# Layer norms of a two-layer decoder step: scaling in place on VectorE, the shift inside the split, GpSimd's shift of the residual later

## The chip, the cores and the metric

The kernel runs on one core of one Trainium2 chip. The metric is the device time of one execution in microseconds (us), the median of several runs. Engines are called PE (TensorE matmuls), DVE (VectorE), ACT (ScalarE), POOL (GpSimd) and SP (SyncE, which issues most DMAs).

## The reference, cut to what matters

One inference step of a decoder with two layers, 512 prompt tokens and 8 single sample tokens, model width 1024, all in float32. Layer 0 mixes tokens by windowed attention, layer 1 by gated linear attention; each is followed by a gated convolutional feed-forward part of width 2816. Behind each of the four parts stands a layer norm of the residual:

```
def layer_norm(x, g, b):
    mu = jnp.mean(x, -1, keepdims=True)
    var = jnp.mean(jnp.square(x - mu), -1, keepdims=True)
    return (x - mu) * lax.rsqrt(var + LN_EPS) * g + b

for i in range(DEPTH):
    x = layer_norm(ALPHA * x + mix_i(x), ln_mix_g[i], ln_mix_b[i])
    x = layer_norm(ALPHA * x + conv_ffn_i(x), ln_ffn_g[i], ln_ffn_b[i])
```

So the result of a norm is used twice: as the input of the next matrix products, and as the residual that the next part is added to.

## The kernel before, in words

**Tiling.** Activations lie with features on the 128 partitions and tokens in the free dimension. The tokens are two groups: a with 256 prompt tokens, b with 256 prompt and 8 sample tokens. A group's residual is the tile x (x_a, x_b): 8 chunks of 128 features. Matrix products run in float32r with operands split in two: a high half, rounded by ACT, and a low half, the rest, by a subtraction on DVE (tiles xh and xl; for group a both lie in xs_a). A product (lines 164 to 195) of one unit, 128 output features by one group, adds high x high, high x low and low x high over the chunks in one of four PSUM accumulators (accp). Weights come by DMA as raw, ACT makes wh (line 158) and DVE wl (line 161).

**Order.** Units are traced in an order in which group a leads group b by four or five units (line 931), so that at the end of a phase b's last units run while a's layer norm is made, and a's first units of the next phase run while b's layer norm is made. One unit of one group is a slot. A generator that yields n is taken up again n slots later (lines 912 to 929). A planner then orders each engine's instructions: it simulates the program with a cost model and takes what is ready, by the order of tracing. `issue_after(ins)` puts what is traced under it behind `ins` in the queue of the same engine; the engines run their queues strictly in order.

**The layer norm.** `ln_chunk` (line 208) adds the last product of a part to chunk m of x and gathers the sums s1 and s2 (of x and its squares). `ln_end` (line 251) is one slot later: PE sums over the partitions by ones matrices (line 256), ACT copies the mean mu (line 261), POOL subtracts it from chunks 0 to 4 and DVE from 5 to 7 (line 263), ACT's Ln and Exp (lines 273, 274) with three DVE operations (275 to 277) give r, the reciprocal deviation. Then for each chunk: DVE multiplies by r into a tile u with two buffers (296), ACT makes the high half from u with gain and shift (297), POOL makes the new residual x from u with gain and shift (298), and DVE subtracts the high half from that x for the low half (301). `pool_mark` is POOL's last such operation; the next norm's subtractions on POOL are issued after it (264). The last norm of the program (`last`) goes another way and writes y.

**The feed-forward part.** `ffn_gate` (line 564) copies a gate product to SBUF with two columns of history in front (POOL copies them, line 202), makes the convolution on DVE (lines 580, 581) and a Gelu on ACT (line 588); `ffn_value` multiplies it with the value product (line 600), which releases that accumulator. The residual x is next touched by `ffn_down` of the first part (line 613), 12 units of each group later, or, in the linear attention, by the output projection (line 219). There POOL also adds one to the denominators of the output gate (line 859).

Of the kernel before, what the change touches and what calls it, by code (L numbers as in the profile page):

```python
# [11 lines left out]
F32 = mybir.dt.float32  # L12
F32R = mybir.dt.float32r
I32 = mybir.dt.int32
AF = mybir.ActivationFunctionType
ALU = mybir.AluOpType
# [6 lines left out]
KD = 8  # L23
# [28 lines left out]

S2P = 4
NSUB = 5

WIDE = 4

# [16 lines left out]
def parted(rows):  # L74

    return rows.rearrange("p (j t) -> p t j", t=2)
# [15 lines left out]
class Net:  # L92
# [157 lines left out]

    def ln_end(self, g, i, last=False):
        nc, n, x = self.nc, g.n, g.x
        yield 1
        e1, e2 = self.mtile("tp")[:, :n], self.mtile("pv")[:, :n]
        for e, sums, rest in ((e1, g.s1, x[:, KD - 1]), (e2, g.s2, g.q)) if last else ((e1, g.s1, None), (e2, g.s2, None)):
            nc.tensor.matmul(e, self.ones_a, sums, start=True, stop=rest is None)
            if rest is not None:
                nc.tensor.matmul(e, self.ones_a, rest, start=False, stop=True)
        t = lambda name, b=1: self.ln.tile([P, NT - 256], F32, name=name, bufs=b)[:, :n]
        mu, q, nv, r = t("mu"), t("msq"), t("nv"), t("r")  # L260
        nc.scalar.copy(mu, e1)
        nc.scalar.activation(q, e1, AF.Square)
        sub = lambda eng, m: eng.tensor_tensor(x[:, m], x[:, m], mu, op=ALU.subtract)
        with self.tc.issue_after(self.pool_mark) if self.pool_mark else ExitStack():
            for m in range(2, KD) if last else range(NSUB):
                sub(nc.gpsimd, m)
        nvi = nc.vector.scalar_tensor_tensor(nv, q, LN_EPS, e2, op0=ALU.subtract, op1=ALU.subtract)
        with self.tc.issue_after(nvi.ins):
            if last:
                nc.vector.tensor_tensor(x[:, 0:2], x[:, 0:2], mu.unsqueeze(1).broadcast_to([P, 2, n]), op=ALU.subtract)  # L270
            else:
                sub(nc.vector, NSUB)
        nc.scalar.activation(r, nv, AF.Ln, scale=-1.0)
        nc.scalar.activation(r, r, AF.Exp, scale=-0.5)
        nc.vector.tensor_tensor(q, r, r, op=ALU.mult)
        nc.vector.scalar_tensor_tensor(q, q, 0.5, nv, op0=ALU.mult, op1=ALU.mult)  # L276
        ri = nc.vector.scalar_tensor_tensor(r, q, 1.5, r, op0=ALU.add, op1=ALU.mult)
        sc = lambda m: self.par[:, C_LNG + i * KD + m:C_LNG + i * KD + m + 1]
        bi = lambda m: self.par[:, C_LNB + i * KD + m:C_LNB + i * KD + m + 1]
        if last:  # L280
            for m in range(0, KD, 2):
                xp = x[:, m:m + 2]
                nc.vector.tensor_tensor(xp, xp, r.unsqueeze(1).broadcast_to([P, 2, n]), op=ALU.mult)
                for j in (m, m + 1):
                    if j in (0, 2, 4, 5, 7):
                        nc.scalar.activation(x[:, j], x[:, j], AF.Identity, scale=sc(j), bias=bi(j))
                    else:
                        nc.vector.tensor_scalar(x[:, j], x[:, j], sc(j), bi(j), op0=ALU.mult, op1=ALU.add)
                nc.sync.dma_start(out=self.O["y"][:, m:m + 2, g.c0:g.c0 + n], in_=xp)
            return  # L290
        for m in range(KD):
            if m > NSUB:
                with self.tc.issue_after(ri.ins):
                    sub(nc.vector, m)
            u = t("u", 2)
            nc.vector.tensor_tensor(u, x[:, m], r, op=ALU.mult)  # L296
            nc.scalar.activation(g.xh[:, m], parted(u), AF.Identity, scale=sc(m), bias=bi(m))
            ts = nc.gpsimd.tensor_scalar(x[:, m], u, sc(m), bi(m), op0=ALU.mult, op1=ALU.add)  # L298
            if m == KD - 1:
                self.pool_mark = ts.ins  # L300
            nc.vector.tensor_tensor(g.xl[:, m], parted(x[:, m]), g.xh[:, m].bitcast(F32), op=ALU.subtract)  # L301

    def load_x(self, i, m0, m1):
        g, nc = self.groups[i], self.nc
# [259 lines left out]
    def ffn_gate(self, g, u, layer, j, q):  # L564
        nc, n = self.nc, g.n
        ps, lo = self.product2(g, u, g.xs, g.xh, g.xl, j >= WIDE)
        w = lambda i: self.par[:, C_CW + (layer * 3 + i) * NF + j:C_CW + (layer * 3 + i) * NF + j + 1]
        cb = self.par[:, C_CB + layer * NF + j:C_CB + layer * NF + j + 1]
        a = self.fp.tile([P, 2 + NT - 256], F32, name="aext", bufs=2)
        if g.i == 0:  # L570
            nc.gpsimd.memset(a[:, 0:2], 0.0)
        else:
            self.pcopy(a[:, 0:2], self.hist[:, j])
        nc.scalar.copy(a[:, 2:2 + n], ps)
        t = lambda name: self.fp.tile([P, NT - 256], F32, name=name, bufs=2)
        c = t("conv")
        if lo is not None:
            nc.vector.tensor_tensor(a[:, 2:2 + n], a[:, 2:2 + n], lo, op=ALU.add)  # L578
        nc.scalar.activation(c[:, :256], ps[:, :256] if lo is None else a[:, 2:258], AF.Identity, scale=w(2), bias=cb)
        nc.vector.scalar_tensor_tensor(c[:, :256], a[:, 1:257], w(1), c[:, :256], op0=ALU.mult, op1=ALU.add)  # L580
        nc.vector.scalar_tensor_tensor(c[:, :256], a[:, 0:256], w(0), c[:, :256], op0=ALU.mult, op1=ALU.add)
        if g.i == 0:
            self.pcopy(self.hist[:, j], a[:, 256:258])
        else:
            nc.vector.scalar_tensor_tensor(c[:, 256:n], a[:, 258:2 + n], w(2), self.base[:, j], op0=ALU.mult, op1=ALU.add)
            self.pcopy(self.nconv_p[:, j], a[:, 256:258])
            self.pcopy(self.nconv_s[:, j, :, 1], a[:, 258:2 + n])
        nc.scalar.activation(c[:, :n], c[:, :n], AF.Gelu)
        g.gate = c
        yield 0  # L590

# [368 lines left out]
    def run(self):  # L960
        nc = self.nc
        self.plan()
        self.nu, self.extra, self.close_wx = WSLOTS, {}, False
        self.attn_open()
        self.later, self.slot, self.seq, self.pool_mark = [], 0, 0, None
        for i, u in self.order():
            g = self.groups[i]
            _, _, f, a, pre = self.units[u]
            if i == 0 and pre:
                pre()  # L970
                if pre != self.gla_open:
                    for _ in range(EXTRA):
                        self.next_unit(True)
            self.slot += 1
            self.resume(f(g, u, *a))
            if i == 1:
                x = self.extra.pop(u, False)
                if not x or self.more(u):
                    self.next_unit(x)
                elif not self.extra:  # L980
                    self.close_wx = True
            if self.close_wx and self.fp is None:
                self.close(self.wx_cm)
                self.close_wx = False
            self.due()
        while self.later:
            self.slot += 1
            self.due()
# [115 lines left out]
```

## Time and profile before

| | us |
|---|---|
| median of 3 timed runs | 1148.62 (1147.16 to 1149.75) |
| the profiled execution | 1146.73 |
| its span in the profile | 1144.7 |
| PE busy | 1104.2 (96%) |
| DVE busy | 794.5 (69%) |
| ACT busy | 575.6 (50%) |
| POOL busy | 326.4 (29%) |

The profile is of one execution. An engine's busy time is the union of its instructions; times of day are counted from the start of the span. The mean granted TensorE clock of the span was 0.992 of full speed. The views used below are the busy time of each engine in windows, the waits (who waited for whose instruction, and how long in all), the chain of work that ended last, the timeline of one engine, and the instructions of one line.

### The profile page before, as it was taken

The page shows a single profiled execution, that of the slowest core. Times are in us where ns is not written, and L with a number is a line of the kernel's source. Part 1 is how long each engine was busy: PE and PEld are TensorE (multiplying, and loading weights), DVE is VectorE, ACT ScalarE, POOL GpSimd, SP SyncE. Part 2 cuts the span into 40 slices and gives each one's busy share as a digit, 9 for nine tenths or more (in the row PEclk, how much of TensorE's full clock was granted, in tenths as well). Part 3 has the DMA queues.
Part 4 walks back from the last instruction along what each step waited for, and adds up shares of the span by engine and source line. Part 5 has one row for each costly group of instructions (what it writes and reads, how often), then busy time and mean ns, then how long its engine had stood idle before and what let it go on. Part 6 is the DMA issues. An engine that isn't in the chain of part 4 may idle for free.

```text
span 1144.7 us, 22953 instructions
## 1 busy us (share of the span) xinstructions
PE 1104.2 (96%) x8806; PEld 1055.2 (92%) x8806; DVE 794.5 (69%) x1663; ACT 575.6 (50%) x1253; POOL 326.4 (29%) x556
## 2 busy tenths in 40 slices
PE   8999899999999999999899999989999999999995
PEld 8997798999999999998899999888999999999994
DVE  7897589655665566668867777799655665566657
ACT  5677457534553245435545556456524553245433
POOL 4575568100110011357300101287100110011344
PEclk9999999999999999999899999999999999999998
DMA  7553031323323233243124355341333232232222
GB/s 241 149 183 90 13 111 56 111 93 123 99 93 111 92 99 105 74 133 110 38 89 147 117 177 162 133 145 62 105 96 127 93 106 98 92 111 93 74 63 75
DMA packets 53789, 122.82 MB, mean 107 GB/s; under 512 B 6792, under 2 KB 27312, under 8 KB 53680
## 3 DMA queue, kind: packets, MB, share of 16 engines
q1 hardware_dynamic: 51664, 119.61, 32.4%
q10 hardware_dynamic: 2016, 1.75, 0.5%
q8 instruction: 69, 1.13, 0.4%
q14 instruction: 40, 0.33, 0.1%
HBM read 108.67 MB, written 8.47 MB: 102 GB/s over the span
## 4 chain that ended last, share of the span: by engine, by line
PE 70%; DVE 12%; DMA 6%; ACT 4%; POOL 4%; issue 4%; SPq 0%; ACTq 0%; DVEq 0%; POOLq 0%
PE accp L191 15%; PE accp L174 14%; PE accp L173 14%; PE accp L175 14%; PE accp L192 8%; DMA vb<-dv 3%; DVE wl L161 2%; POOL x_b L298 1%; DVE sgla L845 1%; DMA qs<-hl 1%; ACT wh L158 1%; POOL x_a L298 1%; DVE u L296 1%; PE pv L494 1%; DVE msq L276 1%
## 5 line engine op out<-in xcount | busy, mean ns | idle before, releaser
L161 DVE TENSOR_TENSOR wl<-raw,wh 128x1024 fp32r<-128x1024 f32 (+2 forms) x189 | 231.4, 1226 | 106.7 <-ACT wh L158 105.2
L158 ACT ACTIVATE wh<-raw 128x1024 fp32r<-128x1024 f32 (+2 forms) x185 | 191.9, 1037 | 215.0 <-PE accp L174 196.8
L173 PE MATMUL accp<-xh_b,wh 128*128 128x264 f32 x976 | 271.7, 279 | 2.5 <-DVE hprod L600 2.5
L174 PE MATMUL accp<-xl_b,wh 128*128 128x264 f32 x976 | 271.3, 278 | 0.2
L175 PE MATMUL accp<-xh_b,wl 128*128 128x264 f32 x976 | 270.8, 278 | 0.0
L191 PE MATMUL accp<-xs_a,wh 128*128 128x512 f32 x576 | 196.3, 382 | 0.0
L173 PEld LDWEIGHTS accp<-xh_b,wh 128*128 128x128 f32 x976 | 185.0, 190 | 3.5 <-DVE hprod L600 2.9
L174 PEld LDWEIGHTS accp<-xl_b,wh 128*128 128x128 f32 x976 | 184.9, 189 | 3.1 <-DVE xl_b L301 0.6
L175 PEld LDWEIGHTS accp<-xh_b,wl 128*128 128x128 f32 x976 | 184.8, 189 | 0.8 <-issue 0.6
L192 PE MATMUL accp<-xs_a,wl 128*128 128x256 f32 x576 | 145.4, 273 | 0.0
L173 PE MATMUL accp<-hh_b,wh 128*128 128x264 f32 x480 | 133.7, 279 | 3.3 <-ACT hh_b L198 3.3
L174 PE MATMUL accp<-hl_b,wh 128*128 128x264 f32 x480 | 134.3, 280 | 0.0
L175 PE MATMUL accp<-hh_b,wl 128*128 128x264 f32 x480 | 133.3, 278 | 0.0
L191 PEld LDWEIGHTS accp<-xs_a,wh 128*128 128x128 f32 x576 | 109.1, 189 | 11.4
L173 PE MATMUL accp<-xs_a,wh 128*128 128x256 f32 x400 | 112.3, 287 | 5.6 <-DVE x_b L219 2.1
L174 PE MATMUL accp<-xs_a,wh 128*128 128x256 f32 x400 | 112.4, 283 | 3.2 <-DVE xs_a L301 2.9
L192 PEld LDWEIGHTS accp<-xs_a,wl 128*128 128x128 f32 x576 | 110.2, 191 | 1.9
L175 PE MATMUL accp<-xs_a,wl 128*128 128x256 f32 x400 | 111.0, 280 | 0.7 <-DVE wl L161 0.5
L173 PEld LDWEIGHTS accp<-hh_b,wh 128*128 128x128 f32 x480 | 91.3, 190 | 3.8 <-ACT hh_b L198 3.6
L174 PEld LDWEIGHTS accp<-hl_b,wh 128*128 128x128 f32 x480 | 91.3, 190 | 1.4 <-issue 0.3
L175 PEld LDWEIGHTS accp<-hh_b,wl 128*128 128x128 f32 x480 | 91.3, 190 | 0.2
L202 POOL COPY hist<-aext 128x2 f32<-128x2 f32 x44 | 8.9, 203 | 284.4 <-DVE aext L578 281.3
(320 smaller groups left out, 2495.3 us busy)
## 6 DMA issues: line engine op xcount, KB each, us to landing
raw<-in_w_up SPq DMA_DIRECT2D x88, 512.0 KB, 3.4
raw<-in_w_down SPq DMA_DIRECT2D x32, 512.0 KB, 3.4
raw<-in_w_gla SPq DMA_DIRECT2D x24, 512.0 KB, 3.4
raw<-in_w_mix_o SPq DMA_DIRECT2D x16, 512.0 KB, 4.1
raw<-in_w_down SPq DMA_DIRECT2D x16, 384.0 KB, 3.1
qs<-hl SPq DMA_DIRECT2D x64, 64.0 KB, 2.1
sgla<-in_state_gla SPq DMA_DIRECT2D x16, 256.0 KB, 2.8
vb<-dv SPq DMA_DIRECT2D x16, 256.0 KB, 3.7
```

Source lines behind the costliest of these rows:

```text
L158: nc.scalar.activation(h[:, c], r[:, c], AF.Copy)
L161: nc.vector.tensor_tensor(l[:, c], r[:, c], h[:, c].bitcast(F32), op=ALU.subtract)
L173: nc.tensor.matmul(o, h[:, ks], xh, start=k == 0, stop=False)
L174: nc.tensor.matmul(o, h[:, ks], xl, start=False, stop=False)
L175: nc.tensor.matmul(o, l[:, ks], xh, start=False, stop=k == nt - 1)
L191: both = lambda: nc.tensor.matmul(o, h[:, ks], in_turn(rs[:, k].rearrange("p t q j -> p t (q j)")), start=k == 0, stop=last)
L192: low = lambda: nc.tensor.matmul(o[:, :P], l[:, ks], in_turn(rh[:, k]), start=False, stop=False)
L276: nc.vector.scalar_tensor_tensor(q, q, 0.5, nv, op0=ALU.mult, op1=ALU.mult)
L296: nc.vector.tensor_tensor(u, x[:, m], r, op=ALU.mult)
L298: ts = nc.gpsimd.tensor_scalar(x[:, m], u, sc(m), bi(m), op0=ALU.mult, op1=ALU.add)
L494: mm = nc.tensor.matmul(pv[64 * v:64 * v + 64, b * P:(b + 1) * P], self.vtok[:, kb, 64 * v:64 * v + 64], parts[v][w][:, b], start=i == 0, ...
L845: late(nc.vector.scalar_tensor_tensor(s[:, j], vb[:, j], kraw[:, b:b + 1], s[:, j], op0=ALU.mult, op1=ALU.add))
```

## The change

In the norms that are not the last, the tile u goes. DVE multiplies x in place by gain and r in one operation; ACT makes the high half from x with the shift as its bias; DVE makes the low half as (x + shift) - high half. POOL adds the shift to x in place in a generator step that is taken up 14 slots later. POOL's mean subtractions are no longer issued after a mark. Group b's `ln_end` is taken up in the same slot, not one later. The Gelus of the first three gates of each feed-forward part are issued after the latest Exp of a norm.

```diff
+LATEB = 14
@@ ln_end
-        yield 1
+        yield 0 if g.i and not last else 1
...
-        with self.tc.issue_after(self.pool_mark) if self.pool_mark else ExitStack():
-            for m in range(2, KD) if last else range(NSUB):
-                sub(nc.gpsimd, m)
+        for m in range(2, KD) if last else range(NSUB):
+            sub(nc.gpsimd, m)
...
-        nc.scalar.activation(r, r, AF.Exp, scale=-0.5)
+        self.exp = nc.scalar.activation(r, r, AF.Exp, scale=-0.5).ins
...
         for m in range(KD):
             if m > NSUB:
                 with self.tc.issue_after(ri.ins):
                     sub(nc.vector, m)
-            u = t("u", 2)
-            nc.vector.tensor_tensor(u, x[:, m], r, op=ALU.mult)
-            nc.scalar.activation(g.xh[:, m], parted(u), AF.Identity, scale=sc(m), bias=bi(m))
-            ts = nc.gpsimd.tensor_scalar(x[:, m], u, sc(m), bi(m), op0=ALU.mult, op1=ALU.add)
-            if m == KD - 1:
-                self.pool_mark = ts.ins
-            nc.vector.tensor_tensor(g.xl[:, m], parted(x[:, m]), g.xh[:, m].bitcast(F32), op=ALU.subtract)
+            nc.vector.scalar_tensor_tensor(x[:, m], x[:, m], sc(m), r, op0=ALU.mult, op1=ALU.mult)
+            nc.scalar.activation(g.xh[:, m], parted(x[:, m]), AF.Identity, bias=bi(m))
+            nc.vector.scalar_tensor_tensor(g.xl[:, m], parted(x[:, m]), bi(m), g.xh[:, m].bitcast(F32), op0=ALU.add, op1=ALU.subtract)
+        yield LATEB
+        for m in range(KD):
+            nc.gpsimd.tensor_scalar(x[:, m], x[:, m], 1.0, bi(m), op0=ALU.mult, op1=ALU.add)
@@ ffn_gate
-        nc.scalar.activation(c[:, :n], c[:, :n], AF.Gelu)
+        with self.tc.issue_after(self.exp) if j < 3 else ExitStack():
+            nc.scalar.activation(c[:, :n], c[:, :n], AF.Gelu)
```

## Rows read from the trace of the kernel before

**Rows 1.** Windows: length, busy PE, PEld, DVE, ACT, POOL (instructions), granted clock, DMA share, GB/s.
```profile
160.00:180.00 20.00, 17.65 (x151) 17.14 (x150) 19.37 (x38) 12.13 (x20) 15.24 (x13) 1.00 0.39 129
180.00:200.00 20.00, 18.24 (x155) 17.45 (x154) 17.81 (x38) 13.84 (x29) 16.65 (x23) 1.00 0.09 27
200.00:220.00 20.00, 20.00 (x160) 19.39 (x159) 14.93 (x30) 11.59 (x22) 3.23 (x12) 1.00 0.38 120
...
520.00:540.00 20.00, 17.51 (x148) 16.82 (x147) 19.07 (x39) 11.97 (x21) 15.25 (x13) 1.00 0.40 132
540.00:560.00 20.00, 16.79 (x109) 14.96 (x109) 16.37 (x37) 11.21 (x24) 11.77 (x14) 0.83 0.03 7
...
760.00:780.00 20.00, 16.64 (x139) 15.90 (x138) 20.00 (x38) 12.21 (x20) 16.38 (x13) 1.00 0.37 126
780.00:800.00 20.00, 18.25 (x154) 17.48 (x153) 17.82 (x38) 13.89 (x29) 16.50 (x23) 1.00 0.09 27
```

**Rows 2.** PE's waits, grouped: us in total, times, the longest.
```profile
PE accp L174 <- DVE xs_a L301: 2.9, 2, 1.5
PE accp L173 <- DVE hprod L600: 2.5, 2, 1.3
PE accp L173 <- DVE x_b L219: 2.1, 2, 1.1
...
PE accp L672 <- DVE xl_b L301: 1.5, 2, 1.0
PE accp L672 <- DVE xs_a L301: 1.3, 1, 1.3
PE accp L173 <- DVE x_b L217: 1.1, 1, 1.1
```

**Rows 3.** The chain that ended last, from 150 to 205: start, us, what.
```profile
191.44 4.12 POOL x_b L298 x4
```

**Rows 4.** POOL's timeline, 155 to 200: start, us, what, idle before and its releaser.
```profile
166.75 6.39 POOL L298 TENSOR_SCALAR x_a<-u,par 128x256 f32<-128x256 f32 x4 [3.22 <-DVE u L296]
...
177.82 3.08 POOL L298 TENSOR_SCALAR x_a<-u,par 128x256 f32<-128x256 f32 x2 [0.70 <-DVE u L296]
180.87 4.33 POOL L263 TENSOR_TENSOR x_b<-x_b,mu 128x264 f32<-128x264 f32 x5
```

**Rows 5.** DVE's timeline, the same stretch.
```profile
166.22 0.76 DVE L296 TENSOR_TENSOR u<-x_a,r 128x256 f32<-128x256 f32 x2
166.89 1.22 DVE L161 TENSOR_TENSOR wl<-raw,wh 128x1024 fp32r<-128x1024 f32 x1
...
169.26 0.43 DVE L301 TENSOR_TENSOR xs_a<-x_a,xs_a 128x256 fp32r<-128x256 f32 x1 [0.47 <-POOL x_a L298]
...
171.03 1.42 DVE L161 TENSOR_TENSOR wl<-raw,wh 128x1024 fp32r<-128x1024 f32 x1
```

**Rows 6.** Line 301: what DVE, idle before it, waited for (us, times).
```profile
  POOL x_a L298: 2.1, 5
  POOL x_b L298: 0.8, 2
```

**Rows 7.** Instructions of lines 580, 277, 298, 558: min/median/max ns, first to last start.
```profile
L580 DVE SCALAR_TENSOR_TENSOR conv<-aext,par,conv x88: 473/482/617, 186.4 to 1091.8; 128x256 f32<-128x256 f32 x88
...
L277 DVE SCALAR_TENSOR_TENSOR r<-msq,r x8: 412/847/873, 164.9 to 1134.9; 128x256 f32<-128x256 f32 x4, 128x264 f32<-128x264 f32 x4
...
L298 POOL TENSOR_SCALAR x_b<-u,par x24: 651/1110/1322, 186.3 to 794.9; 128x264 f32<-128x264 f32 x24
...
L558 POOL TENSOR_TENSOR base<-sconv,par x2: 495/534/573, 140.4 to 755.1; 128x176 f32<-128x176 f32 x2
```

**Rows 8.** ACT's timeline, 155 to 200.
```profile
177.45 0.38 ACT L261 COPY mu<-tp 128x264 f32<-128x264 f32 x1 [0.45 <-PE tp L256]
...
180.37 0.42 ACT L274 ACTIVATE r<-r 128x264 f32<-128x264 f32 x1
...
187.47 1.28 ACT L588 ACT_TABLE_LOAD   x1
```

More of the change, by code (lines that the diff above doesn't have):

```diff
@@ L964, in run @@
         self.attn_open()
-        self.later, self.slot, self.seq, self.pool_mark = [], 0, 0, None
+        self.later, self.slot, self.seq = [], 0, 0
         for i, u in self.order():
```

## The prediction

> **What bounds the kernel now.** The first view to read is the busy time by windows of 20 us, TensorE (PE) first. In the middle of a feed-forward phase PE is busy for 20.00 of 20 us while VectorE (DVE) has some 25% left [rows 1], as in the window from 200. PE loses time in three places: 160 to 200, 520 to 560 and 760 to 800, with 4.11, 5.70 and 5.11 us not busy (20 minus the PE column, summed over two windows), together 14.9 us. In the window from 540 the granted clock is also 0.83 on average: with two levels that is 6.8 of the 20 us at the lower, 1.2 GHz (0.17 / 0.5 x 20), which costs up to 3.4 us of matmul time. DVE is at 16.4 to 20.0 of 20 us there. So about 18 us is all that there is to win at these places. They are the three layer norms that are not the last, each for group a and then for group b.
>
> Second, PE's waits, grouped [rows 2]. Three kinds carry these places: waits that end with the low half of a normalized chunk (L301: 2.9, 1.5 and 1.3, in sum 5.7 us), waits for an accumulator that the gate-times-value product has to release (L600, 2.5 us), and waits for one that the residual add has to release (L219 and L217, 2.1 and 1.1 us). All end on DVE.
>
> Third, what DVE waits for. Across the first layer norm the chain of waits runs through GpSimd (POOL): four of its scalings (L298) in a row make up 4.12 us of it [rows 3]. POOL's own timeline says why [rows 4]: beside a busy DVE four scalings take 6.39 us, 1.6 each, and the subtractions of the mean for group b begin at 180.87, when group a's last scaling ends, because line 264 puts them behind it. Group a's first chunk is multiplied by r at 166.22 and its low half starts only at 169.26, DVE having sat idle 0.47 us for POOL [rows 5]. Over all layer norms DVE idled 2.9 us in front of L301 for L298 [rows 6].
>
> **The change part by part.**
> (a) The low half no longer reads what POOL wrote. Per chunk there were, and are, two DVE operations and one on ScalarE (ACT); POOL's scaling leaves the chain between them, and so does the two-buffer tile u. Group a's first chunk took 3.04 us from 166.22 to 169.26; the two DVE operations (0.4 us each) with ACT's (0.6) between them would take half of that. I count the whole of the 5.7 us that PE waited for L301. From below this could be 0, if DVE's backlog lets nothing come earlier; from above it is 5.7.
> (b) Group b's mean subtractions are no longer behind group a's scalings. POOL could start when the mean is there, at 177.83 (177.45 and 0.38 us [rows 8]), where two scalings of group a now start [rows 4]: 3.0 us before 180.87. That moves group b's chunks and, with them off DVE, the convolutions and products of the first gates: the 2.5 us of waits for L600 go. Bounds: 0 (r of group b comes from DVE, not from POOL) and 2.5.
> (c) The waits for the residual add stay as they are, 3.2 us: they come from the order in DVE's queue.
> (d) The stretch at the lower clock followed stop-and-go matmuls. With part of those stops gone I take half of it, 1.7 us. Bounds 0 and 3.4; the nearest rows say no more than that one of the three places has it and the two others don't [rows 1].
> (e) The price: both new DVE operations take a per-partition operand from the parameter tile. A scalar_tensor_tensor of 128x256 took at least 0.473 us with such an operand (L580) and 0.412 with a constant (L277) [rows 7]; the tensor_tensor that they replace is as quick as the latter, 0.76 us for two that overlap [rows 5]. That is 0.061 us more for each of 2 operations x 8 chunks x 6 norms = 96, or 5.9 us of DVE time. Where DVE is full half of it reaches PE by my reckoning: 2.9 us. Bounds 0 and 5.9.
> (f) POOL's 48 operations come back 14 slots later and change x in place. Alone or beside DVE they take 0.65 to 1.3 us (L298 on group b) [rows 7], so some 53 us of POOL in all, and they slow DVE a little: splitting weights took 1.22 us and 1.42 us in two places beside such scalings [rows 5], so up to 0.2 each, 9.6 us of DVE. They are not wanted before x is next added to, in the first down projection or the next output projection. If they land after the window, PE is at 20.00 of 20 there and DVE's free quarter hides them; if the planner pulls them forward, the contention is what it is today. Zero, with 9.6 as the price if DVE had no room.
> (g) Group b's statistics matmuls are written one slot earlier. DVE's sums, not the slot, release them, so zero; a slot, about 24 matmuls at 20/160 us [rows 1], is 3 us, the most that it could give or take.
> (h) The Gelus of the first three gates are put behind the layer norm's Exp in ACT's queue. They are behind it already: Exp at 180.37, the Gelu table at 187.47 [rows 8]. Zero; the cover is 7 us wide, and if it went two more table loads of 1.28 us would be at stake in each feed-forward phase. In the last norm only the order behind an old mark goes: zero.
>
> The sum: -5.7 - 2.5 - 1.7 + 2.9 = -7.0 us. The profiled execution took 1146.73 us (span 1144.7, 2.0 outside), so 1139.7 for such a one; the median of the timed runs is 1.9 above it, so 1141.6 there. By each part's bounds the likeliest case lies between -11.6 and 0; I expect it within 1137 to 1146.
>
> The Trainium skill speaks against (f). Its GPSIMD Engine Reference, under Key points, says that GpSimd shares its SBUF interfaces with VectorE and contends with VectorE instructions that have two SBUF inputs. The trace agrees: 1.6 us a scaling beside DVE in rows 4 against 0.65 at best in rows 7. By that rule moving the scalings into the feed-forward phase, where DVE has many two-input operations, keeps their cost rather than removing it; the sum above does not credit any relief for it.
>
> **The rivals.**
> R1, no change: DVE's total work is the bound and only the order of it changes. For it: DVE is within 0 to 1 us of full in the windows from 160, 520 and 760 [rows 1], and (e) adds 5.9 us against the 2.9 us of idle time that it loses [rows 6] and what the missing waits let it do. Then the time is 1148.6 plus or minus 2: +3.0 of DVE, less about as much as is put off until after the place, where DVE has room. Against it: the weight splits of 1.2 us in these places aren't needed at once, and can wait.
> The Trainium skill has a rule on R1's side: VectorE: DVE Perf Modes, under Rules for kernel authors, advises to cut the number of DVE operations rather than fuse them. Here 96 stand for 96; by that rule DVE gains nothing. No row can show the new pair itself.
>
> R2, slower: the late scalings block POOL's queue. They are issued eight at a time per group; if the eight stand together, 8 x 1.11 us (median of L298 on group b [rows 7]) = 8.9 us during which the tiny copies of the gate's history, or the denominators of the linear attention's gate, stand behind them, DVE waits in order for those, and PE's accumulators are not released. Of four accumulators two are filled or read, so the other two give about 2 x 3.0 = 6 us of cover. The excess, 2.9 us, comes six times: +17.4, less 7, is +10.4, so 1159. It decides only from a block longer than six us. Against it: the planner puts POOL operations where POOL is idle. The feed-forward phase's base computation (L558) first ran at 140.4 [rows 7], 26 us before group a's first normalized chunk at 166.22 [rows 5], which opens that phase; and POOL is busy for only 3 of 20 us behind the place [rows 1].
>
> R3, faster still: the chunks are ready so early that the planner puts off weight splits and nearly all of the three places closes. Of the 14.9 us and 3.4 of clock, three quarters: -13.7, so 1135. For it: POOL's pace is 1.6 us a chunk today and DVE's would be 0.8. Against it: (c), and DVE at 20.
>
> **How the numbers follow.** The forecast (1137 to 1146) gets 0.52, R3 0.17, R1 0.18, R2 0.13. About 0.2%, 2.3 us, is what a measurement of this kernel can tell from no change. Below 1146.3 lie the forecast, R3 and a sixth of R1: 0.72. Above 1150.9 lies R2 and a trace of R1: 0.14. The rest, 0.14, is no change. The range from 1133 to 1151 takes in the forecast, R1 and most of R3 and leaves out R2: some 0.8.
>
> **What would show it.** Right: no wait of PE or DVE that ends at POOL's scaling; group b's mean subtractions on POOL right behind the mean, some 3 us earlier than now; PE busy 37 to 39 of 40 us in 160 to 200 and 760 to 800; the waits for L301 and L600 under 3 us together; no stretch, or a shorter one, at 0.5 clock near 550; the new DVE operations at 0.47 to 0.49 us. Wrong: the same PE stalls ending at DVE operations of another line (R1), or DVE and PE waiting for a POOL copy behind a row of eight scalings in the feed-forward phases (R2). The prediction is wrong if the three places don't shrink, or if PE falls below 19.9 of 20 in the windows right behind them.

## The result, and the profile after

Before 1148.59 us (1147.16 to 1150.63, 6 runs), after 1154.26 us (1153.72 to 1155.44, 6 runs): a ratio of 1.0048, 95% interval 1.0035 to 1.0061. By the ratio the kernel became slower by 5.5 us, where 7 us less were forecast. The profiled execution of after took 1154.34 us, its span 1152.2 (7.5 more than before) at a mean granted clock of 0.983.

The changed kernel's lines are shifted a little: L297 is the multiplication in place, L298 ACT's high half, L299 the low half, L302 POOL's later shift, L249 and L251 the sums of group b, L163 the weight split, L263 the copy of the mean, L265 the mean subtraction, L221 the residual add, L603 the gate product.

The windows of after, in the columns of [rows 1]:

```profile
160.00:180.00 20.00, 16.64 (x123) 16.45 (x122) 19.46 (x37) 11.08 (x19) 11.00 (x14) 0.83 0.32 106
180.00:200.00 20.00, 19.25 (x165) 18.73 (x165) 16.43 (x37) 11.16 (x25) 8.93 (x12) 1.00 0.17 53
200.00:220.00 20.00, 20.00 (x166) 19.58 (x165) 15.46 (x29) 13.02 (x26) 8.67 (x22) 1.00 0.36 113
520.00:540.00 20.00, 16.20 (x138) 15.71 (x137) 19.19 (x36) 11.95 (x22) 9.44 (x11) 1.00 0.31 105
540.00:560.00 20.00, 16.36 (x124) 15.25 (x123) 17.50 (x38) 7.40 (x19) 11.75 (x16) 0.95 0.09 28
560.00:580.00 20.00, 18.43 (x138) 17.64 (x138) 14.90 (x34) 11.18 (x28) 1.61 (x4) 0.88 0.21 70
760.00:780.00 20.00, 15.37 (x119) 14.88 (x118) 19.67 (x35) 11.69 (x22) 12.06 (x15) 0.91 0.33 106
780.00:800.00 20.00, 19.46 (x155) 18.97 (x154) 16.53 (x36) 11.52 (x25) 9.89 (x16) 0.92 0.26 79
```

The same three places are open, and the first window of each opened further: PE is 3.36 us short of full from 160 (2.35 before), 3.80 from 520 (2.49) and 4.63 from 760 (3.36), while the second window of the first and third closed by about 1 us (0.75 against 1.76 from 180). New is the granted clock there, 0.83 and 0.91 where it had been 1.00. From 200 on PE is at 20.00 of 20 as before; behind the second norm the loss runs on into the window from 560 (18.43, where it had been 20.00). Comparing when the same DVE instruction starts in both traces says the same: after is 1.2 us late ahead of the first norm, gains 1.8, 2.3 and 2.2 us of lateness at the three norms, and stays constant through the feed-forward phases between them (3.06 us late from 252 to 500). The 1.2 us lie in attention, in front of the first changed instruction, and are less than the 1.9 us by which the profiled execution of before was under its median; part of them goes with the clock, 0.72 on average from 132 to 144 where before had 0.86.

PE's waits of after, grouped, in the columns of [rows 2]:

```profile
PE accp L176 <- DVE xs_a L299: 7.3, 2, 3.9
PE accp L675 <- DVE xs_a L299: 3.8, 2, 3.4
PE accp L675 <- DVE xl_b L299: 3.6, 2, 2.8
```

The waits for the gate product and the residual add of [rows 2] have gone, and DVE no longer sits idle in front of a low half (2.1 and 0.8 us for POOL in [rows 6]). But the wait for the low half went from 5.7 us in all to 14.7, and the longest from 1.5 to 3.9. What DVE does in front of it, to hold against [rows 5]:

```profile
167.45 2.85 DVE L297 SCALAR_TENSOR_TENSOR x_a<-x_a,par,r 128x256 f32<-128x256 f32 x7
170.22 1.21 DVE L163 TENSOR_TENSOR wl<-raw,wh 128x1024 fp32r<-128x1024 f32 x1
171.36 0.47 DVE L297 SCALAR_TENSOR_TENSOR x_a<-x_a,par,r 128x256 f32<-128x256 f32 x1
171.75 0.42 DVE L249 TENSOR_TENSOR s_b<-s_b,x_b 128x264 f32<-128x264 f32 x1
172.10 0.42 DVE L251 TENSOR_TENSOR s_b<-s_b,sq 128x264 f32<-128x264 f32 x1
172.44 0.47 DVE L299 SCALAR_TENSOR_TENSOR xs_a<-x_a,par,xs_a 128x256 fp32r<-128x256 f32 x1
```

Before, two multiplications were issued (x2 in [rows 5]) and then none until ACT and POOL had read one of u's two buffers. The third stands behind the first low half (169.26 in [rows 5]):

```profile
169.60 0.42 DVE L296 TENSOR_TENSOR u<-x_a,r 128x256 f32<-128x256 f32 x1
```

Now seven stand in one row, then a weight split, the eighth, two sums of group b, and only then the first low half: 4.99 us behind the first multiplication instead of 3.04. DVE has no idle time in this stretch: it is not waiting for anyone, it does other work first. ACT had the first two high halves done by 168.92:

```profile
167.96 0.96 ACT L298 ACTIVATE xs_a<-x_a,par 128x256 fp32r<-128x256 f32 x2
...
185.32 0.38 ACT L263 COPY mu<-tp 128x264 f32<-128x264 f32 x1
```

With the long stops the clock fell. Windows of after cut at the changes of clock:

```profile
165.30:172.10 6.80, 4.31 (x39) 4.12 (x37) 6.80 (x17) 3.67 (x8) 0.00 (x0) 1.00 0.25 81
172.10:178.90 6.80, 5.93 (x28) 5.94 (x29) 6.80 (x15) 3.66 (x7) 5.14 (x7) 0.50 0.49 154
...
776.30:783.10 6.80, 5.97 (x28) 5.98 (x29) 6.80 (x15) 2.15 (x4) 5.18 (x7) 0.50 0.50 157
```

For 6.8 us PE ran at 0.50, 1.2 GHz, and did 28 matmuls where the same stretch of before holds 48:

```profile
172.10:178.90 6.80, 5.81 (x48) 5.58 (x48) 6.80 (x16) 5.14 (x9) 5.26 (x4) 1.00 0.48 154
```

How much of the loss is the clock's was not separated. At the second norm the low clock lasts no longer than before (0.95 and 0.88 in two windows against 0.83 in one, 6.8 us in either case), and 2.3 us were lost there all the same. Last, POOL, to hold against [rows 4]:

```profile
160.53 4.23 POOL L265 TENSOR_TENSOR x_a<-x_a,mu 128x256 f32<-128x256 f32 x5
173.02 0.48 POOL L302 TENSOR_SCALAR x_a<-x_a,par 128x256 f32<-128x256 f32 x1 [8.26 <-DVE xs_a L299]
...
175.62 5.18 POOL L302 TENSOR_SCALAR x_a<-x_a,par 128x256 f32<-128x256 f32 x6 [0.37 <-DVE xs_a L299]
...
185.79 4.15 POOL L265 TENSOR_TENSOR x_b<-x_b,mu 128x264 f32<-128x264 f32 x5 [0.65 <-ACT mu L263]
```

The planner pulled the later shifts forward, directly behind the low halves. Group b's mean subtractions start at 185.79, 4.9 us later than before, because the mean itself comes at 185.32 (177.45 before [rows 8]). Of these 7.9 us DVE makes 4.6: group b's last sum, behind the multiplications and low halves in its queue, ends at 181.42 (176.85 before). The rest is PE's, which has products of group a in front of the statistics matmuls and starts those at 184.62 (176.75 before).

### The profile page after: what moved, and what is told of

It reads as the page before. It is cut to its first block, busy times and chain, and to the rows that moved or that the text cites. A ratio compares the mean times of both kernels' runs of the same rounds, so it can differ in the third digit from the quotient of the medians.

```text
span 1152.2 us, 22899 instructions
## 1 busy us (share of the span) xinstructions
PE 1106.8 (96%) x8806; PEld 1058.7 (92%) x8806; DVE 797.0 (69%) x1663; ACT 568.3 (49%) x1253; POOL 301.3 (26%) x556
## 4 chain that ended last, share of the span: by engine, by line
PE 76%; DVE 11%; DMA 5%; ACT 3%; issue 2%; POOL 1%; SPq 1%; ACTq 0%; DVEq 0%; POOLq 0%
PE accp L176 16%; PE accp L175 16%; PE accp L177 16%; PE accp L193 15%; PE accp L194 8%; DMA vb<-dv 2%; DVE wl L163 2%; DMA raw<-in_w_qkv 1%; DMA qs<-hl 1%; DVE x_a L297 1%; DVE sgla L848 1%; ACT wh L160 1%; PE pv L495 1%; DVE x_b L297 1%; ACT pr L464 1%
## 5 line engine op out<-in xcount | busy, mean ns | idle before, releaser
L163 DVE TENSOR_TENSOR wl<-raw,wh 128x1024 fp32r<-128x1024 f32 (+2 forms) x189 | 230.3, 1220 | 107.8 <-ACT wh L160 107.1
L176 PE MATMUL accp<-xs_a,wh 128*128 128x256 f32 x400 | 113.5, 286 | 7.8 <-DVE xs_a L299 7.3
L193 PEld LDWEIGHTS accp<-xs_a,wh 128*128 128x128 f32 x576 | 109.1, 189 | 11.4
L175 PE MATMUL accp<-xs_a,wh 128*128 128x256 f32 x400 | 114.6, 290 | 2.2 <-ACT wh L160 0.8
L176 PEld LDWEIGHTS accp<-xs_a,wh 128*128 128x128 f32 x400 | 78.9, 198 | 9.2 <-DVE xs_a L299 7.7
```

Source lines behind the costliest of these rows:

```text
L163: nc.vector.tensor_tensor(l[:, c], r[:, c], h[:, c].bitcast(F32), op=ALU.subtract)
L175: nc.tensor.matmul(o, h[:, ks], xh, start=k == 0, stop=False)
L176: nc.tensor.matmul(o, h[:, ks], xl, start=False, stop=False)
L193: both = lambda: nc.tensor.matmul(o, h[:, ks], in_turn(rs[:, k].rearrange("p t q j -> p t (q j)")), start=k == 0, stop=last)
```

## The experiments

Three theories were tested. T1: the order of DVE's queue, which the two buffers of u had set, costs the time. T2: the per-partition operand of the two new DVE operations costs it. T3: POOL's later operations cost it, by contention or by blocking its queue. Ratios are to the kernel before on the same chip; the intervals are 95%.

**The order put back (e1).** The changed kernel, with the multiplication of chunk m issued behind the low half of chunk m-2, as it stood with the two buffers:

```diff
+        lows = []
...
-            nc.vector.scalar_tensor_tensor(x[:, m], x[:, m], sc(m), r, op0=ALU.mult, op1=ALU.mult)
+            with self.tc.issue_after(lows[m - 2]) if m >= 2 else ExitStack():
+                nc.vector.scalar_tensor_tensor(x[:, m], x[:, m], sc(m), r, op0=ALU.mult, op1=ALU.mult)
...
-            nc.vector.scalar_tensor_tensor(g.xl[:, m], parted(x[:, m]), bi(m), g.xh[:, m].bitcast(F32), op0=ALU.add, op1=ALU.subtract)
+            lo = nc.vector.scalar_tensor_tensor(g.xl[:, m], parted(x[:, m]), bi(m), g.xh[:, m].bitcast(F32), op0=ALU.add, op1=ALU.subtract)
+            lows.append(lo.ins)
```

> The changed kernel, with one edge more: DVE's multiplication of chunk m is issued behind the low half of chunk m-2, so multiplications and low halves alternate again as the two buffers of u made them do before; instructions, operands and POOL's late step are those of the changed kernel. T1 (order: eight multiplications ahead of the first low half make PE stop once for 3.5 to 4 us at each norm, and the clock falls for 6.8 us): the long stops and the half-clock stretches at the three norms go, 1140 to 1149, at least 5 us under the changed kernel. T2 (the per-partition operands, 5.9 us more DVE work): still 1152 to 1156. T3 (late POOL operations contend or block): still 1152 to 1156.

Measured 1150.23 us, ratio 1.0012 (1.0000 to 1.0023): about 4 of the 5.5 us come back. That lies between T1's range (up to 1149, at least 5 us less) and that of T2 and T3 (from 1152): the order is most of the loss, not all of it. DVE's queue in it (the multiplication is L299 here, the low half L301):

```profile
167.69 0.86 DVE L299 SCALAR_TENSOR_TENSOR x_a<-x_a,par,r 128x256 f32<-128x256 f32 x2
168.49 1.21 DVE L163 TENSOR_TENSOR wl<-raw,wh 128x1024 fp32r<-128x1024 f32 x1
...
170.31 0.47 DVE L301 SCALAR_TENSOR_TENSOR xs_a<-x_a,par,xs_a 128x256 fp32r<-128x256 f32 x1
170.71 0.47 DVE L299 SCALAR_TENSOR_TENSOR x_a<-x_a,par,r 128x256 f32<-128x256 f32 x1
...
181.52 0.97 DVE L301 SCALAR_TENSOR_TENSOR xs_a<-x_a,par,xs_a 128x256 fp32r<-128x256 f32 x1
```

The first low half comes 2.62 us behind the first multiplication, and the windows of the first and third norm are back at a granted clock of 1.00:

```profile
160.00:200.00 40.00, 35.82 (x296) 33.98 (x295) 38.59 (x76) 23.39 (x45) 28.71 (x34) 1.00 0.24 80
...
760.00:800.00 40.00, 34.44 (x282) 32.43 (x281) 38.90 (x76) 23.09 (x45) 30.07 (x35) 1.00 0.24 79
```

At the second norm it is as before (0.94 from 520 to 580 in both).

PE's waits for group a's low half are 3.8 us in eight pieces of at most 1.6, and the gate product and the residual add are waited for again:

```profile
PE accp L176 <- DVE xs_a L301: 3.8, 8, 1.6
...
PE accp L175 <- DVE hprod L606: 2.5, 2, 1.3
...
PE accp L175 <- DVE x_b L221: 1.8, 2, 0.9
```

**The buffers alone taken away (e2).** The kernel before, with one edit:

```diff
-            u = t("u", 2)
+            u = x[:, m]
```

> The kernel before, with u replaced by x itself (multiplied in place) and nothing else: no per-partition operand on DVE, POOL's scaling in the chain at once, POOL's subtractions behind the mark. T1: the planner puts the multiplications first here too; slower than before, 1151 to 1158, with a stop of over 3 us at the first low half. T2 and T3: as before, 1147 to 1150.

Measured 1162.21 us, ratio 1.0112 (1.0099 to 1.0125), above the range that T1 gave. This kernel still has the old operations, POOL in the chain and the mark; only the multiplication is in place. DVE's queue took the form of after:

```profile
167.23 2.42 DVE L296 TENSOR_TENSOR x_a<-x_a,r 128x256 f32<-128x256 f32 x7
169.58 1.21 DVE L161 TENSOR_TENSOR wl<-raw,wh 128x1024 fp32r<-128x1024 f32 x1
170.72 0.41 DVE L296 TENSOR_TENSOR x_a<-x_a,r 128x256 f32<-128x256 f32 x1
...
171.74 0.41 DVE L219 SCALAR_TENSOR_TENSOR x_b<-x_b,accp 128x264 f32<-128x264 f32 x1
172.28 0.42 DVE L301 TENSOR_TENSOR xs_a<-x_a,xs_a 128x256 fp32r<-128x256 f32 x1
```

T1's direction is shown: the same order of multiplications, and a loss, 12.9 us, that is larger than T1 put. The stop of over 3 us at the first low half, which T1 named, is not there. PE waits for the residual add that stands behind the multiplications and just ahead of that low half, and later for group b's high half:

```profile
PE accp L173 <- ACT xh_b L297: 6.3, 2, 3.2
PE accp L173 <- DVE x_b L219: 6.1, 2, 3.3
```

The edit also does more than take buffers away. POOL now overwrites the x that ACT reads, so its first scaling waits for ACT's high half (3.92 us idle at the first norm), where in before it waited for DVE's u (3.22 in [rows 4]). So the 12.9 us are the order and this further wait together. The rest of the change gives 7 us of them back (1.0112 against 1.0048).

**The gain left out (e3).** The changed kernel with the constant 1.0 in place of the gain, so that the multiplication has no per-partition operand; the order is that of after:

```diff
-            nc.vector.scalar_tensor_tensor(x[:, m], x[:, m], sc(m), r, op0=ALU.mult, op1=ALU.mult)
+            nc.vector.scalar_tensor_tensor(x[:, m], x[:, m], 1.0, r, op0=ALU.mult, op1=ALU.mult)
```

> The changed kernel with the constant 1.0 in place of the gain in the multiplication (the gain is left out): that operation costs 0.41 us instead of 0.47, 48 times, 2.9 us of DVE in all; DVE's order is the same. T1: within 2 us of the changed kernel, 1152 to 1155, stops of 3 us and half clock still there. T2: 2.5 to 3 us faster than the changed kernel, 1151 to 1152. T3: 1154.

Measured 1152.66 us, ratio 1.0026 (1.0017 to 1.0035): 2.5 us under after by the ratios, which is T2's price (2.5 to 3) and just beyond what T1 alone allowed (2). The long stops stay, as T1 says, and each is 0.4 to 0.5 us shorter than in after, as eight multiplications of 0.41 instead of 0.47 us stand in front of it:

```profile
PE accp L176 <- DVE xs_a L299: 6.4, 2, 3.5
```

**POOL's step not put off (e4).**

```diff
-LATEB = 14
+LATEB = 0
```

> The changed kernel with 0 slots in place of 14 before POOL adds the shift. T1 and T2: 1153 to 1156, as the planner pulls these operations forward in either case. T3 (their place matters): over 3 us away from 1154, up or down.

Measured 1156.16 us, ratio 1.0055 (1.0042 to 1.0069), the same as after within the intervals. POOL's timeline has the eight shifts behind the low halves as in after: the number of slots does not decide where they go, so this run moved nothing and cannot price another place. Against T3 speaks e1. There too the shifts follow the low halves at once, and DVE's low halves of group a take as long beside them as in after (0.61 and 0.60 us on average), yet 4 us come back. What POOL's late operations cost in both was not taken alone.

**Order back and both operands constant (e5).** e1 with constants in both new operations; gain and the shift of the low half are left out:

```diff
+                nc.vector.scalar_tensor_tensor(x[:, m], x[:, m], 1.0, r, op0=ALU.mult, op1=ALU.mult)
...
+            lo = nc.vector.scalar_tensor_tensor(g.xl[:, m], parted(x[:, m]), 0.0, g.xh[:, m].bitcast(F32), op0=ALU.add, op1=ALU.subtract)
```

> e1_pairs with constants for both new operands on DVE: 1.0 for the gain in the multiplication and 0.0 for the shift in the low half (both are left out there), so each of the 96 operations costs 0.41 instead of 0.47 us; the alternating order stays. T1 with T2's price added (order undone, the per-partition operands cost 3 to 5 us and eat what the missing POOL step gives): 3 to 5 us under e1_pairs and under the kernel before, 1144 to 1147. T1 alone (order is all, operands hidden): within 1 us of e1_pairs, 1149 to 1151.

Measured 1148.0 us, ratio 0.9992 (0.9982 to 1.0001). That is 2.3 us under e1 and less than was expected; no more of the price shows with two operands constant than e3 had with one. So order and operand price together account for the loss against before, but even without both the change wins next to nothing. PE now waited for the gate product:

```profile
PE accp L175 <- DVE hprod L606: 5.6, 2, 3.1
```

The clock fell at the first and third norm again, to 0.96 from 160 to 200 and 0.91 from 760 to 800 (1.00 in e1), so the 2.3 us are net of that.

**The weight splits moved (e6, e7, e8).** What remains in DVE's backlog are the weight splits of 1.2 us. In e6 (e1 plus this) and e7 (before plus this) the splits traced after a group a norm are issued behind its last low half, in e8 (e1 plus this) behind its fourth, with `m == 3` below:

```diff
+            with self.tc.issue_after(self.hold) if self.hold else ExitStack():
                 nc.vector.tensor_tensor(l[:, c], r[:, c], h[:, c].bitcast(F32), op=ALU.subtract)
...
+            if m == 7 and not g.i:
+                self.hold = lo.ins
```

> e1_pairs, and DVE's splits of weights (1.2 us each) that are traced after group a's norm are issued behind its last low half. If DVE's backlog sets the pace at the norms, the splits ahead of the low halves are what PE waits for: first low half 2 us earlier, 1142 to 1147. If something else does (POOL, ACT, the order of the rest): 1149 to 1151. If PE needs those weights soon: over 1152, with waits for wl.

> The kernel before with the same edge for the splits of weights and nothing of the change. If the backlog of DVE and not the change is what there is to win: 1143 to 1147, as good as e6_pairs_wl. If POOL's scaling in the chain holds the low halves once the splits are out of the way: 1147 to 1150, 2 us or more behind e6_pairs_wl.

> e6_pairs_wl with the splits behind the low half of chunk 3 in place of chunk 7: between e1_pairs and e6_pairs_wl if the backlog is the cause, 1143 to 1149; faster than e6_pairs_wl by 1 to 2 us if PE needs the weights early there.

Measured e6 1147.68, 0.9989 (0.9978 to 1.0000); e7 1147.31, 0.9989 (0.9977 to 1.0000); e8 1149.01, 0.9996 (0.9986 to 1.0006). Against e1 the splits give 2.6 us, against before 1.3, and with them both kernels come to the same time. e6 and e7 lie just above the ranges that a backlog on DVE was given (up to 1147), e8 between e1 and e6 as that theory has it; and POOL's scaling in the chain does not put e7 2 us behind e6, as the other theory had it. The waits for the low halves turn into waits for the splits. In e6:

```profile
PE accp L178 <- DVE wl L164: 5.9, 8, 1.9
```

In e7:

```profile
PE accp L176 <- DVE wl L162: 4.7, 8, 1.3
```

That fits one backlog on DVE, for whose pieces PE waits in whatever order they are worked off. e6 and e7 are the lowest of all, by an amount at the edge of what can be told from no change.

**The two written-order edits undone (e9).** e1 with `yield 1` for both groups and the Gelus without their place behind Exp:

```diff
-        yield 0 if g.i and not last else 1
+        yield 1
...
-        with self.tc.issue_after(self.exp) if j < 3 else ExitStack():
-            nc.scalar.activation(c[:, :n], c[:, :n], AF.Gelu)
+        nc.scalar.activation(c[:, :n], c[:, :n], AF.Gelu)
```

> The kernel with the multiplications in pairs with the low halves, and the two written-order parts of the change undone as well: group b's statistics matmuls again one slot later, and the first three Gelus without their place behind Exp. Prediction terms (g) and (h): both were put at zero, so the time is that of e1_pairs, 1.0012 of before, within 0.15%. Rival: one of them carries part of the 1.4 us that e1_pairs stays above before; then this comes to 0.9990 to 1.0003. Other rival: the slot was a gain (up to 3 us in a norm at most by the bound), then 1.002 to 1.006.

Measured 1151.36, ratio 1.0018 (1.0004 to 1.0032), the same as e1: together the two edits are worth nothing that can be measured, as put down in (g) and (h). The interval leaves room for some 2 us of gain by them, and the two were not taken apart.

**POOL's mark alone taken away (e10).** The kernel before, with one edit:

```diff
-        with self.tc.issue_after(self.pool_mark) if self.pool_mark else ExitStack():
-            for m in range(2, KD) if last else range(NSUB):
-                sub(nc.gpsimd, m)
+        for m in range(2, KD) if last else range(NSUB):
+            sub(nc.gpsimd, m)
```

> The kernel before, with only the order of GpSimd's queue freed: group b's mean subtractions no longer behind group a's last scaling. Prediction term (b) taken alone: up to 2.5 us faster, 0.9978 of before, the waits for the gate product (2.5 us) gone. Theory after the result: VectorE's backlog bounds group b (the sums and the eighth, sixth and seventh subtraction are VectorE's own), so 0.999 to 1.001, the waits for the gate product stay. Rival: the freed subtractions come ahead of group a's last scalings and keep PE waiting for group a's low halves, 1.001 to 1.005.

Measured 1155.8, ratio 1.0055 (1.0039 to 1.0071). Neither (b) nor the theory written after the result; it is the rival, a little beyond its range. POOL's timeline in it (the scaling is L297 here):

```profile
179.95 1.97 POOL L297 TENSOR_SCALAR x_a<-u,par 128x256 f32<-128x256 f32 x1 [0.71 <-DVE u L295]
181.89 4.62 POOL L263 TENSOR_TENSOR x_b<-x_b,mu 128x264 f32<-128x264 f32 x5
186.50 1.25 POOL L297 TENSOR_SCALAR x_a<-u,par 128x256 f32<-128x256 f32 x1
```

The five subtractions go ahead of group a's last scaling, DVE makes the eighth low half only at 187.78, and PE waits up to 3.5 us for low halves (16.3 us in all):

```profile
PE accp L174 <- DVE xs_a L300: 11.4, 6, 3.4
PE accp L671 <- DVE xs_a L300: 4.9, 2, 3.5
```

The clock falls there too, to 0.55 from 188 to 195:

```profile
188.00:195.00 7.00, 6.74 (x34) 6.74 (x35) 6.36 (x17) 5.89 (x12) 6.29 (x10) 0.55 0.01 2
```

So the mark shielded the old chain. In e1, where the low half no longer reads what POOL wrote, the five subtractions again go ahead of three operations for group a (180.41 against 184.88), and no wait of PE or DVE ends at those.

## Why the prediction was wrong, point by point

**(a), the step that failed:** "I count the whole of the 5.7 us that PE waited for L301." It took u's two buffers as a cost in the chain, and not as what set DVE's order. With two buffers at most two multiplications could be ahead of the low halves; without them they need only r and the mean subtracted, while each low half needs ACT first, and the planner put all eight in front. Why it did not take the first low half once ACT's high half was done (168.92) no run shows. The wait rose to 14.7 us. e1 shows it: the pairing put back takes the ratio from 1.0048 to 1.0012. e2, where the same order came into the old kernel together with a further wait of POOL's, gives 1.0112. [Rows 5] had the sign: the multiplications stand there as x2, and [rows 4] have POOL waiting for `u`.

The estimate for the first chunk, half of the 3.04 us, left out what else stands in DVE's queue. Even in pairs (e1) it was 2.62, since the weight split and two sums stand between.

**(b)** failed. The 2.5 us of waits for the gate product did go in after, but in e1 they are back. Group b's subtractions came later, not earlier: the mean hangs on DVE's sums. With the pairs of e1 they start at 180.41, 0.5 us earlier and not 3. The mark was not what cost group b time: taken away in the old kernel it costs 6.3 us (e10).

**(c)** was put at no change; the waits for the residual add went from the list in after, where the longer stop stands. In e1 they are there again, 1.8 us and a further 1.0.

**(d)** had the wrong sign: instead of half a stretch less there are two more, of 6.8 us each, right at the long stops, and the one at the second norm stays. In e1 the two are gone. The Trainium skill (TensorE: Matmul & The Clock Gate, Loop structure matters more than you think) gives a long DMA wait in front of every matmul as the case in which PE's clock falls to half. The rows agree on the clock, 0.50 from 172.10 and from 776.30, but the waits here were for DVE and came once at a norm.

**(e)** was right in the least price of one operation; the sum fits better than its reckoning. The lines of the two new operations in after, beside [rows 7]:

```profile
L297 DVE SCALAR_TENSOR_TENSOR x_a<-x_a,par,r x24: 468/471/473, 167.5 to 775.5; 128x256 f32<-128x256 f32 x24
```

And the low half:

```profile
L299 DVE SCALAR_TENSOR_TENSOR xs_a<-x_a,par,xs_a x24: 469/638/704, 172.4 to 782.0; 128x256 fp32r<-128x256 f32 x24
```

At least 0.47 us, as taken from L580. The multiplications keep to that; the low halves, beside POOL's shifts, have a median of 0.64 in group a, above the 0.47 to 0.49 named as a sign. Constants bring 2.5 us in the order of after (e3, one of the two operations) and 2.3 in pairs (e5, both), against the 2.9 forecast for both. By the forecast's own half, e3 should have brought 1.5 and e5 2.9; and DVE's busy time rose by 2.5 us in all (797.0 against 794.5), not by 5.9.

**(f)** zero fits: PE is at 20.00 of 20 in the window from 200, and the lateness does not grow in the feed-forward phases. It came about by the second case that (f) named: the planner pulled the shifts forward. The contention stayed about what it was, as (f) said for that case: group a's low half takes 0.60 us on average, 0.13 above its least, where before it was 0.52 and 0.11 above. **(g), (h)** zero fits for the two together (e9).

**The sum and the signs.** "By each part's bounds the likeliest case lies between -11.6 and 0" leaves out the upper bound of (e), 5.9 us. With it the parts' own bounds take in the measured 5.5, though not by way of (e) alone: 4 of them came with the order (e1), and (a) had 0 as its worst case. Of the signs of being right, one came: no wait ends at POOL's scaling. PE was busy 35.9 and 34.8 of 40 us at the first and third norm where 37 to 39 were named, and behind the second, from 560, it fell to 18.43 where 19.9 was the limit.

**The rivals.** R2 is not seen: behind group b's norm seven shifts stand in a row on POOL (6.43 us from 196.80), but no wait of DVE or PE ends at one of POOL's small copies there. The slower outcome had another mechanism, which was not among the rivals. R3 fell with (a). R1's mechanism, that DVE's total work is the bound and only its order changes, fits what is left when the order is set right: e1 lies in R1's range (1148.6 plus or minus 2), and e5, without the price, at 0.9992. The Trainium skill (VectorE: DVE Perf Modes, Rules for kernel authors) advises to lower the number of DVE operations and not to fuse them for speed. These runs agree: 96 for 96 bring nothing.

Four things stay open: why the planner put all eight multiplications first; how the loss divides between the stops and the low clock that follows them; what the 7 us are made of that the rest of the change gives back against e2; and how much of e5's 2.3 us is the operands', since its queue is not quite e1's and its clock fell.

## What to carry to other kernels

A rotating buffer in a kernel whose order a planner makes is also a throttle: before removing it, ask which instructions all become ready at once and what then stands behind them in an in-order queue. Where an engine shows no idle time in the stretch, as DVE here, taking one of its releasers out of the chain need not gain anything; look at the work on that engine and at what stands first in its queue. An ordering edge that looks like a cost should be taken away alone before its removal is counted as a gain.

## What the runs showed of the hardware that was not expected

DVE operations beside POOL's subtractions with two tensor inputs took up to twice as long, more than the 0.2 us each that the prediction allowed for a neighbour. In e1 the low half takes 0.47 us at 170.31, where POOL is idle, and 0.97 at 181.52, while POOL subtracts group b's mean:

```profile
180.41 4.49 POOL L265 TENSOR_TENSOR x_b<-x_b,mu 128x264 f32<-128x264 f32 x5
```

The clock followed the long stops: waits of 3.4 and 3.9 us at the low halves of the first and third norm of after went with 6.8 us at half clock each, while the stops of at most 1.6 us at the same two places in e1 left it at 1.00. The length of the longest stop does not settle it, though. In e9, whose longest stop at the third norm was 1.6 us too, the clock from 760 to 800 was 0.96.
